# RWKV inputs: mixtures in the order of their use, r as plain fp32 products, three raw and three split weight buffers, finished chunks turned first

## Chip, cores and metric

The kernel runs on one core of a Trainium2 chip. The metric is the device time of one execution in microseconds (us), from the first to the last instruction with what lies around them; a kernel's figure is the median of its timed runs. TensorE has two clock levels, 1.2 and 2.4 GHz; the profile gives the granted clock of a stretch as a share of 2.4 GHz (1.00 or 0.50, and values between where a stretch holds both).

## The reference

Two blocks of two layers work on a sequence of 256 tokens by 1024 features, in float32. The first block (convolution mixer, cross attention, dense and mixture-of-experts feed-forward) and the first layer of the second block (attention, feed-forward) are untouched by the change. The change lies in the second layer of the second block, an RWKV-7 mixer that runs over the sequence in both directions:

```python
def rwkv7_mixer(h, ...):
    dx_p = jnp.pad(h, ((0, 0), (1, 0), (0, 0)))[:, :-1] - h
    dx_n = jnp.pad(h, ((0, 0), (0, 1), (0, 0)))[:, 1:] - h
    def mix(c):
        return h + dx_p * mu_prev[c] + dx_n * mu_next[c]
    xw, xa, xg = mix(1), mix(4), mix(5)
    r = mix(0) @ w_r
    k = mix(2) @ w_k
    v = mix(3) @ w_v
    kk = heads(k * k_k); kk = kk / norm(kk)
    for d in range(2):
        w_log = -softplus(-(w0[d] + tanh(xw @ w1[d]) @ w2[d])) - 0.5
        a = sigmoid(a0[d] + (xa @ a1[d]) @ a2[d])
        g = sigmoid(xg @ g1[d]) @ g2[d]
        ...   # scan over the tokens, group norm, bonus, times g
    y = dir_out[0] + dir_out[1]
    return y @ w_o
```

So six mixtures of the normalised input with its two neighbours feed six projections: k (mixture 2), the three low-rank ones w, a, g (mixtures 1, 4, 5), r (mixture 0) and v (mixture 3).

## The kernel before, in words

Features lie on the partitions, 8 tiles of 128 (`KD` = 8), and the 256 tokens in the free dimension. Weights stream from memory in raw chunks of 1024 KB into the pool `wst`.

There are two kinds of projections. A *split* one (`proj_T`, `proj`) cuts each operand in two fp32r parts, high and low, and makes three products for each (line 381); for that, ScalarE writes `wh` (line 344) and VectorE `wl` (line 345) from the raw chunk `wst`, which is free again then. A *plain* one (`plain_T`, line 514) multiplies the fp32 values in one go, with the raw chunk itself as operand, so that the chunk is free when TensorE has read it. The profile records a plain fp32 product of 128x256 as two matmul instructions.

In `rwkv_inputs` the normalised, transposed input is `hT`. A mixture for a plain projection is made by `whole`: for each of the 8 tiles one scaled copy on ScalarE (line 1431) and two multiply-adds on VectorE (line 1433) into `mx`. A mixture for a split projection is made by `mixed`: the same into `mixt` (lines 1444, 1446; four buffers of two tiles), then `mx_h` on ScalarE (line 1448) and `mx_l` on GpSimd (line 1449). The projections come in this order: k (plain), low-rank w (plain), r (split), group norms of k, low-rank a (plain), v (split), low-rank g (plain). After each pair of output tiles of k, ScalarE squares them (`ksq`, line 1461), TensorE sums the squares by group (line 1463), and VectorE and ScalarE write `z0` and `z1`. The order in which each engine issues its instructions comes from a planner that works on a simulated timeline; `high_priority` moves a block ahead in it, and `issue_after(ins)` queues the instructions of a block that run on the engine of `ins` behind `ins` in that engine's order (it adds no wait). `behind` does that for the instructions in the list `turned_all`, which `raw_T` sets.

The pool set `dense("c", 2, 4, "right", 3)` gives this stage two raw buffers `wst`, four each of `wh` and `wl`, and three of the mixture tiles.

After the inputs come the block stage (`rwkv_blocks`: VectorE and GpSimd products, lines 1572 to 1600), the inverses, and four steps of the scan. Step i handles chunk i of 64 tokens in one direction and chunk 3 - i in the other; `rwkv_norm` adds a chunk's normalised output to `y` (lines 1799 to 1801). So chunks 1 and 2 of `y` are complete after step 2, and chunks 0 and 3 after step 3. Then `y` is turned back to features on partitions by 128 small products with the identity (line 1394, `ps_tr`), split into `ry_h` and `ry_l` (lines 372, 373), and projected by `rk_o` (split, into `ps_acc`). The banks of PSUM are tagged: two `mm`, two `tr`, four `acc`; the scan's second direction uses `mm` and `tr`.

Of the kernel before, what the change touches and what calls it, by code (L numbers as in the profile page):

```python
# [15 lines left out]
OP = mybir.AluOpType  # L16
# [5 lines left out]
KD = 8  # L22
S = 256
# [191 lines left out]
class K:  # L215
# [1090 lines left out]
    def rwkv(self, h, hstack, hp):  # L1306
# [4 lines left out]
        nc, tc = self.nc, self.tc  # L1311
        with ExitStack() as ctx:
# [5 lines left out]
            with ExitStack() as left:  # L1318
                with ExitStack() as right:
                    rz = pool(right, "rwz", "right")  # L1320
                    rT, z0, z1 = (rz.tile([P, KD, S], F32, name=n) for n in ("rT", "z0", "z1"))
                    tT = rz.tile([65, 2, S], F32, name="tT")
                    aT = rz.tile([P, S], F32, name="aT")
                    nc.gpsimd.memset(tT[64:65], 1.0)
                    bq = pool(right, "rwq", "right")

                    def opened():
                        hstack.close()
                        lp = pool(ctx, "rwl", "left")
                        return lp, lp.tile([P, KD, 4, 64], F32, name="vx"), lp.tile([P, 2, S], F32, name="gT")  # L1330
                    with self.dense("c", 2, 4, "right", 3):
                        lp, vx, vm, gT = self.rwkv_inputs(h, rT, z0, z1, tT, aT, opened,
                                                      lambda lp: self.rwkv_low(bq, lp, 0, tT, aT))
                    cp = pool(left, "rwc", "left")
                    nt, pc, bon = ([cp.tile(sh, F32, name=f"{n}{d}") for d in range(2)] for n, sh in (
                        ("nt", [P, KD * 4, 64]), ("pc", [P, KD, 4]), ("bon", [P, KD, 4])))
                    xt = [cp.tile([P, KD * 4, 64], F32, name="xt0")]
                    ip = pool(left, "rwi", "left")
                    mp = pool(left, "rwm", "left", 2)
                    bp = pool(right, "rwb", "right")  # L1340
                    pads = [bp.tile([P, 4, 256], F32, name=f"pad{i}") for i in range(3)]
                    for t in pads:
                        nc.gpsimd.memset(t, 0.0)
                    for d in range(2):
                        sga = self.sga if d == 0 else self.rwkv_low(bq, lp, 1, tT, aT)
                        self.rwkv_blocks(bp, d, rT, z0, z1, pads, sga, nt[d], pc[d], bon[d], scr)
                    self.rwkv_inverse(ip, ip.tile([P, 3, 32, 32], F32, name="lanes", tag="lanes"), 0, nt[0], xt[0])
# [36 lines left out]
            with self.dense("d", side="right"):  # L1384
                yT = (self.xp.tile([P, KD, S], F32R, name="ry_h", tag="xT_h"),
                      self.xp.tile([P, KD, S], F32R, name="ry_l", tag="xT_l"))
                for f0 in range(0, KD, 2):
                    b = self.bank("tr")
                    for f in range(2):
                        for c in range(4):  # L1390
                            cs = slice(f * S + c * 64, f * S + c * 64 + 64)
                            for par in range(2):
                                src = slice(64 - 64 * par, 128 - 64 * par)
                                nc.tensor.matmul(b[64 * par:64 * par + 64, cs], y[src, f0 + f, c],  # L1394
                                                 self.ident[src, src], start=True, stop=True,
                                                 skip_group_check=True)
                    self.split(yT[0][:, f0:f0 + 2], yT[1][:, f0:f0 + 2], b.rearrange("p (f s) -> p f s", f=2))
                self.add_normed(self.wk, h, self.proj("rk_o", yT), self.norm2(1, 1))
        return h

    def rwkv_inputs(self, h, rT, z0, z1, tT, aT, opened, low):
# [3 lines left out]
        nc = self.nc  # L1405
        lo_, hi_ = slice(0, 64), slice(64, 128)
        with self.tc.tile_pool(name="rin", bufs=1, side="right", reuse_waits="tile") as mp:
# [20 lines left out]
            def whole(c):  # L1428
                x = self.xp.tile([P, KD, S], F32, name="mx", tag="xT_h")
                for q in range(KD):  # L1430
                    nc.scalar.activation(x[:, q], hT[:, q, 1:S + 1], AF.Copy, scale=mu0[:, c, q:q + 1])
                    for i, mu in ((0, mup), (2, mun)):
                        nc.vector.scalar_tensor_tensor(x[:, q], hT[:, q, i:i + S], mu[:, c, q:q + 1], x[:, q],
                                                       op0=OP.mult, op1=OP.add)
                return x

            def mixed(c):
# [18 lines left out]
            def ev_k(i, b):  # L1456
                nc.scalar.copy(z1[lo_, i:i + 2], b[lo_])
                nc.scalar.copy(z0[hi_, i:i + 2], b[hi_])
                for k in (i, i + 1):
# [4 lines left out]
                                         start=k + t == 0, stop=k == KD - 1, skip_group_check=True)  # L1464
                    for ps, z in ((lo_, z0), (hi_, z1)):
                        nc.vector.tensor_scalar(z[ps, k], b[ps, k - i], kg[ps, k:k + 1], None, op0=OP.mult)
            self.plain_T("rk_k", whole(2), 0, 8, ev_k)

            with self.tc.high_priority(400):
                r = self.rsqrt(pg[:, 0:32], 32, 1.0, 1e-30, op=OP.max)  # L1470
# [2 lines left out]
            def ev_w(i, b):  # L1473
                for d in range(2):
                    nc.scalar.activation(tT[0:64, d], b[64 * d:64 * d + 64, 0], AF.Tanh)
            self.plain_T("rk_l1", whole(1), 0, 1, ev_w)
            self.proj_T("rk_r", mixed(0), 0, 8, lambda i, b: nc.scalar.copy(rT[:, i:i + 2], b))
            for k0, pb in self.by_group(r):
                ks = slice(k0, k0 + 2)
                nc.vector.tensor_mul(z0[lo_, ks], z0[lo_, ks], pb[lo_])  # L1480
# [404 lines left out]
```

## Time and profile before

| | |
|---|---|
| median of 3 runs | 2659.81 us (2658.15 to 2661.5) |
| the profiled execution: its time | 2657.13 us |
| the profiled execution: span from first to last instruction | 2655.3 us |
| mean granted clock of TensorE | 0.949 |
| busy: TensorE, VectorE, ScalarE, GpSimd | 2451.8, 1994.8, 1548.3, 343.3 us |

All times of rows are microseconds from the span's start in that one execution. PE is TensorE (PEld its weight loads), DVE is VectorE, ACT is ScalarE, POOL is GpSimd, SPq the queue of SyncE that issues the transfers. A busy share over the whole span mixes stages with different limits, so stretches are read apart.

### The profile page before, as it was taken

The numbers are of one execution on the slowest core, as the hardware profiler recorded it, in microseconds if no ns is written. First come the engines' busy times: TensorE is split into PE (matmuls) and PEld (weight loads), VectorE is DVE, ScalarE is ACT, GpSimd is POOL, SyncE is SP. The second block draws the span as 40 slices with busy tenths as digits, with TensorE's granted clock in tenths as the row PEclk, the third lists the DMA queues.
The fourth block names the chain that finished last, engine by engine and source line by source line (L and its number), as shares of the span: only waits on it lengthen the run. The fifth ranks groups of instructions, "written<-read, shape, count | busy, mean of one in ns | idle before, by whom it ended". The sixth has DMA issues, their size and how long they took to land. (4 is left out here: it accounts for less than half of the span.)

```text
span 2655.3 us, 41131 instructions
## 1 busy us (share of the span) xinstructions
PE 2451.8 (92%) x15984; PEld 2102.2 (79%) x15984; DVE 1994.8 (75%) x2962; ACT 1548.3 (58%) x2168; POOL 343.3 (13%) x293
## 2 busy tenths in 40 slices
PE   8889999889999999999999999889899698687998
PEld 8778998778788888788888888677798576666897
DVE  8956556956689999888898989766655767867655
ACT  5445445335578777777777777645443446664443
POOL 3800110750000000000000000000011215500111
PEclk9989999899999999999999999989999799779999
DMA  6524454444489999999999999572453335735552
GB/s 243 169 103 148 163 190 164 139 148 175 135 316 368 348 362 353 353 347 358 350 359 345 353 362 362 185 258 80 140 186 104 129 121 126 189 126 203 175 188 98
DMA packets 229960, 598.83 MB, mean 226 GB/s; under 512 B 14779, under 2 KB 33915, under 8 KB 228477
## 3 DMA queue, kind: packets, MB, share of 16 engines
q1 hardware_dynamic: 229756, 596.12, 64.3%
q8 instruction: 127, 2.08, 0.3%
q14 instruction: 77, 0.62, 0.1%
HBM read 579.27 MB, written 16.81 MB: 224 GB/s over the span
## 5 line engine op out<-in xcount | busy, mean ns | idle before, releaser
L345 DVE TENSOR_TENSOR wl<-wst,wh 128x1024 fp32r<-128x1024 f32 (+2 forms) x1025 | 1227.9, 1227 | 347.8 <-ACT wh L344 339.8
L344 ACT ACTIVATE wh<-wst 128x1024 fp32r<-128x1024 f32 (+2 forms) x1025 | 1057.5, 1055 | 523.7 <-PE ps_mm L381 271.5
L381 PE MATMUL ps_mm<-xT_h,wh 128*128 128x256 f32 x1496 | 434.1, 290 | 28.4 <-DVE xT_l L460 15.4
L381 PE MATMUL ps_mm<-xT_h,wl 128*128 128x256 f32 x1496 | 431.2, 288 | 3.6 <-DVE wl L345 2.0
L381 PE MATMUL ps_mm<-xT_l,wh 128*128 128x256 f32 x1496 | 431.5, 288 | 0.2 <-DVE xT_l L460 0.2
L381 PE MATMUL ps_mm<-wh,gh 128*128 128x512 f32 x880 | 349.8, 398 | 0.0
L381 PE MATMUL ps_mm<-wl,gh 128*128 128x512 f32 x880 | 345.1, 392 | 0.0
L381 PE MATMUL ps_mm<-wh,gl 128*128 128x512 f32 x880 | 343.4, 390 | 0.0
L381 PEld LDWEIGHTS ps_mm<-xT_h,wh 128*128 128x128 f32 x1496 | 294.8, 197 | 35.6 <-DVE xT_l L460 16.3
L381 PEld LDWEIGHTS ps_mm<-xT_h,wl 128*128 128x128 f32 x1496 | 294.4, 197 | 7.1 <-DVE wl L345 4.3
L381 PEld LDWEIGHTS ps_mm<-xT_l,wh 128*128 128x128 f32 x1496 | 294.2, 197 | 1.1 <-DVE xT_l L460 0.4
L381 PEld LDWEIGHTS ps_mm<-wl,gh 128*128 128x128 f32 x880 | 165.3, 188 | 36.1
L381 PEld LDWEIGHTS ps_mm<-wh,gl 128*128 128x128 f32 x880 | 165.6, 188 | 32.9
L381 PEld LDWEIGHTS ps_mm<-wh,gh 128*128 128x128 f32 x880 | 165.5, 188 | 32.9
L381 PE MATMUL ps_acc<-wh,mal 128*128 128x512 f32 x448 | 179.0, 400 | 5.5 <-DVE mal L373 5.5
L381 PE MATMUL ps_acc<-wh,mah 128*128 128x512 f32 x448 | 177.7, 397 | 0.7 <-ACT mah L372 0.7
L381 PE MATMUL ps_acc<-wl,mah 128*128 128x512 f32 x448 | 177.6, 396 | 0.0
L1189 POOL MEMSET qz<- 64x2048 f32 x1 | 1.8, 1800 | 1156.3 <-DVEq L935 1156.3
L381 PE MATMUL ps_acc<-wh,al 128*128 128x512 f32 x344 | 134.8, 392 | 0.0
L381 PE MATMUL ps_acc<-wl,ah 128*128 128x512 f32 x344 | 134.5, 391 | 0.0
L1298 POOL TENSOR_TENSOR mq<-mr 128x512 f32<-128x512 f32 x32 | 55.2, 1729 | 582.0 <-DVE mr L1296 582.0
L381 PE MATMUL ps_acc<-wh,ah 128*128 128x512 f32 x344 | 115.9, 396 | 2.5 <-ACT ah L372 2.5
(484 smaller groups left out, 3846.2 us busy)
## 6 DMA issues: line engine op xcount, KB each, us to landing
wst<-in_moe_gate SPq DMA_DIRECT2D x112, 1024.0 KB, 7.0
wst<-in_moe_up SPq DMA_DIRECT2D x112, 1024.0 KB, 7.0
wst<-in_moe_down SPq DMA_DIRECT2D x112, 1024.0 KB, 6.5
wst<-in_mlp SPq DMA_DIRECT2D x64, 1024.0 KB, 4.8
wst<-in_mix_in SPq DMA_DIRECT2D x16, 1024.0 KB, 5.2
mc<-rwscr SPq DMA_DIRECT2D x8, 1792.0 KB, 7.2
wst<-in_ffn_gate SPq DMA_DIRECT2D x11, 1024.0 KB, 4.8
wst<-in_ffn_up SPq DMA_DIRECT2D x11, 1024.0 KB, 5.0
```

The lines of the kernel that those rows point to most:

```text
L344: nc.scalar.activation(wh[:, :n], src, AF.Copy)
L345: nc.vector.tensor_sub(wl[:, :n], src, wh[:, :n])
L381: self.nc.tensor.matmul(out, a, b, start=start and i == 0, stop=stop and i == n - 1, skip_group_check=True)
L1189: nc.gpsimd.memset(qz[64:128, :, 0], 0.0)
L1298: nc.gpsimd.tensor_mul(q, r, r)
```

## The change

Five things are changed. The mixture for k is made ahead under a raised priority, and the one for the low-rank w is traced before k's projection, in a block that queues its VectorE instructions behind the last VectorE step of k's mixture; r's mixture is queued in the same way behind that of w (`whole` now leaves its own last step in `turned_all`). r is a plain projection of a `whole` mixture in place of a split one. The pool set of the stage has three raw and three split buffers in place of two and four. The turn of `y` takes chunks 1 and 2 of all tiles first and chunks 0 and 3 after that, into four banks that are open at once, two tagged `tr` and two `mm`; the splits follow behind all turns in the text of the program. The mixtures of a, v and g are made as before.

```diff
-                    with self.dense("c", 2, 4, "right", 3):
+                    with self.dense("c", 3, 3, "right", 3):
...
-                for f0 in range(0, KD, 2):
-                    b = self.bank("tr")
-                    for f in range(2):
-                        for c in range(4):
-                            cs = slice(f * S + c * 64, f * S + c * 64 + 64)
+                bs = [self.bank(tag) for tag in ("tr", "tr", "mm", "mm")]
+                for cp in ((1, 2), (0, 3)):
+                    for f in range(KD):
+                        for c in cp:
+                            cs = slice(f % 2 * S + c * 64, f % 2 * S + c * 64 + 64)
                             for par in range(2):
                                 src = slice(64 - 64 * par, 128 - 64 * par)
-                                nc.tensor.matmul(b[64 * par:64 * par + 64, cs], y[src, f0 + f, c],
+                                nc.tensor.matmul(bs[f // 2][64 * par:64 * par + 64, cs], y[src, f, c],
                                                  self.ident[src, src], start=True, stop=True,
                                                  skip_group_check=True)
-                    self.split(yT[0][:, f0:f0 + 2], yT[1][:, f0:f0 + 2], b.rearrange("p (f s) -> p f s", f=2))
+                for f0 in range(0, KD, 2):
+                    self.split(yT[0][:, f0:f0 + 2], yT[1][:, f0:f0 + 2],
+                               bs[f0 // 2].rearrange("p (f s) -> p f s", f=2))
...
-                        nc.vector.scalar_tensor_tensor(x[:, q], hT[:, q, i:i + S], mu[:, c, q:q + 1], x[:, q],
-                                                       op0=OP.mult, op1=OP.add)
+                        last = nc.vector.scalar_tensor_tensor(x[:, q], hT[:, q, i:i + S], mu[:, c, q:q + 1], x[:, q],
+                                                              op0=OP.mult, op1=OP.add)
+                self.turned_all = [last]
                 return x
...
-            self.plain_T("rk_k", whole(2), 0, 8, ev_k)
+            with self.tc.high_priority(200):
+                first = whole(2)
+            with self.behind():
+                second = whole(1)
+            self.plain_T("rk_k", first, 0, 8, ev_k)
...
-            self.plain_T("rk_l1", whole(1), 0, 1, ev_w)
-            self.proj_T("rk_r", mixed(0), 0, 8, lambda i, b: nc.scalar.copy(rT[:, i:i + 2], b))
+            self.plain_T("rk_l1", second, 0, 1, ev_w)
+            with self.behind():
+                third = whole(0)
+            self.plain_T("rk_r", third, 0, 8, lambda i, b: nc.scalar.copy(rT[:, i:i + 2], b))
```

## Rows read from the trace of the kernel before

**Rows 1.** The head of the page and its first part: busy time and share.
```profile
span 2655.3 us, 41131 instructions
...
PE 2451.8 (92%) x15984; PEld 2102.2 (79%) x15984; DVE 1994.8 (75%) x2962; ACT 1548.3 (58%) x2168; POOL 343.3 (13%) x293
```

**Rows 2.** Busy time by engine in stretches of the inputs; then clock, DMA share, GB/s.
```profile
2072.00:2085.00 13.00, 5.21 (x13) 2.96 (x13) 13.00 (x34) 4.03 (x10) 8.73 (x1) 0.63 0.06 21
...
2125.00:2139.00 14.00, 8.44 (x42) 7.86 (x43) 11.73 (x23) 3.70 (x4) 4.68 (x4) 0.56 0.37 133
2139.00:2157.00 18.00, 18.00 (x153) 18.00 (x152) 7.24 (x6) 7.81 (x9) 0.00 (x0) 1.00 0.28 102
2157.00:2175.00 18.00, 18.00 (x86) 14.32 (x85) 15.74 (x30) 8.07 (x15) 1.89 (x2) 1.00 0.36 117
2175.00:2189.00 14.00, 14.00 (x56) 9.92 (x55) 4.63 (x8) 5.49 (x11) 0.00 (x0) 1.00 0.43 150
```

**Rows 3.** Timeline of TensorE: start, length, instructions [idle before, releaser].
```profile
2071.62 2.07 PE L514 MATMUL ps_mm<-mx,wst 128*128 128x256 f32 x4 [5.73 <-DVE mx L1433]
...
2076.37 1.13 PE L514 MATMUL ps_mm<-mx,wst 128*128 128x256 f32 x4 [0.31 <-DVE mx L1433]
2084.68 13.89 PE L514 MATMUL ps_mm<-mx,wst 128*128 128x256 f32 x52 [7.18 <-DVE mx L1433]
...
2107.57 7.15 PE L514 MATMUL ps_mm<-mx,wst 128*128 128x256 f32 x32
...
2122.23 0.62 PE L1463 MATMUL ps_tr<-cons,ksq 128*128 128x16 f32 x4 [1.51 <-ACT ksq L1461]
...
2131.72 0.58 PE L381 MATMUL ps_mm<-mx_h,wl 128*128 128x256 f32 x1 [3.33 <-DVE wl L345]
```

**Rows 4.** Waits of TensorE, 2065 to 2205: in total, times, longest.
```profile
PE ps_mm L514 <- DVE mx L1433: 13.5, 4, 7.2
PE ps_mm L381 <- ACT wh L344: 4.4, 2, 3.1
PE ps_mm L381 <- DVE wl L345: 3.3, 1, 3.3
PE ps_tr L1463 <- ACT ksq L1461: 2.6, 2, 1.5
```

**Rows 5.** Timeline of VectorE at the start of the inputs.
```profile
2068.32 0.87 DVE L1433 SCALAR_TENSOR_TENSOR mx<-hT,feats,mx 128x256 f32<-128x256 f32 x2
...
2077.03 3.64 DVE L1433 SCALAR_TENSOR_TENSOR mx<-hT,feats,mx 128x256 f32<-128x256 f32 x9
```

**Rows 6.** VectorE by line, 2065 to 2203: busy, mean ns, idle before.
```profile
L345 DVE TENSOR_TENSOR wl<-wst,wh 128x1024 fp32r<-128x1024 f32 x16 | 19.1, 1220 | 18.8 <-ACT wh L344 18.7
```

**Rows 7.** Transfers issued, 2040 to 2230: size, median us from issue to landing.
```profile
wst<-in_rk_v SPq DMA_DIRECT2D x4, 1024.0 KB, 4.9
```

**Rows 8.** The chain that ended last, 2420 to 2480: start, length, what.
```profile
2422.39 6.25 PE ps_tr L1394 x128
2428.64 22.00 PE ps_acc L381 x96
```

**Rows 9.** Timeline of SyncE's queue at the end of the scan.
```profile
2421.67 2.17 SPq L319 DMA_DIRECT2D wst<-in_rk_o  x4
```

**Rows 10.** Timeline of ScalarE behind the scan.
```profile
2426.63 2.01 ACT L344 ACTIVATE wh<-wst 128x1024 fp32r<-128x1024 f32 x2
```

**Rows 11.** The stretch ahead of the first `rk_o` product, columns as in the second group.
```profile
2426.00:2428.00 2.00, 2.00 (x51) 2.00 (x48) 0.97 (x2) 1.89 (x3) 0.00 (x0) 0.63 1.04 416
```

**Rows 12.** VectorE's products in the block stage, 2203 to 2310, by line and shape.
```profile
L1573 DVE TENSOR_TENSOR bk<-aw,zt 128x256 f32<-128x256 f32 x32 | 17.3, 569 | 0.2
...
L1575 DVE TENSOR_TENSOR pad<-z,e 64x256 f32<-64x256 f32 x16 | 12.8, 803 | 0.4
L1580 DVE TENSOR_TENSOR q<-bk,pad 64x256 f32<-64x256 f32 x16 | 11.1, 698 | 0.4
L1574 DVE TENSOR_TENSOR pad<-z,e 64x256 f32<-64x256 f32 x16 | 9.7, 604 | 5.9 <-issue 3.0 <-ACT e L1560 2.6
```

**Rows 13.** Timeline of GpSimd at the start of the inputs.
```profile
2076.27 11.07 POOL L1449 TENSOR_TENSOR mx_l<-mixt,mx_h 128x512 fp32r<-128x512 f32 x1 [30.09 <-ACT mx_h L1448]
```

## The prediction

> **What bounds the kernel now.** I first read the page: TensorE is busy 92% of a span of 2655.3 us [rows 1], but that is an average over stages. The change touches only the RWKV layer: the projections of `rwkv_inputs` and the turn of `y` ahead of `rk_o`. So I cut the first of these into stretches [rows 2]. From 2139 to 2189 TensorE is busy in every microsecond, at a granted clock of 1.00; it does r's products up to 2157, then group norms, v and small projections. Between 2072 and 2085 it works 5.21 of 13 us, between 2125 and 2139 8.44 of 14, at clocks of 0.63 and 0.56. These two holes are what the change can win; the 32 us after 2157 have none.
>
> The timeline of TensorE says what the holes are [rows 3]. Products of k start at 2071.62 and stop until 2084.68, waiting for VectorE's `mx`. Then they run densely; one chunk of 32 records takes 7.15 us, 0.223 us a record (two records make one fp32 product, here and in all that follows). The last small product after k and the first low-rank projection starts at 2122.23 and takes 0.62 us. Then r waits for split weights and gets going at 2131.72. The waits, summed, are 13.5 us for VectorE's `mx`, 4.4 for ScalarE's `wh` and 3.3 for VectorE's `wl` [rows 4]. The timeline of VectorE shows why the first wait exists [rows 5]: from 2068.32 on the steps of `mx` alternate with steps of `mixt`, and `mx` itself is two mixtures at once, so the one that k needs (16 steps) is spread over three mixtures' 48. One step takes 3.64/9 = 0.404 us when they stand back to back.
>
> **The change, part by part.** *The hold.* k's mixture is issued first, the mixture of the low-rank projection behind it on VectorE, r's behind that. 16 steps x 0.404 = 6.5 us from 2068.3: k's mixture is complete at 2074.8. TensorE can follow it, as it followed the scattered steps before. At 2074.8 all but the last 2 of the 16 records of the first output tile can be done, so 114 of k's 128 records are left. At 2084.68, before, 116 were left (three groups of 4 were done, two of them in [rows 3]). The old stretch from 2084.68 to 2122.85 takes 38.2 us: (116 + 16) x 0.223 = 29.4 us of products, and 8.8 us for the rise of the clock, group sums and waits for squares. I keep the 8.8: with 130 records the stretch takes 37.8 us and ends at 2112.6. Gain: 10.2 us. The hold binds only VectorE instructions; what is queued behind it there are the second and the third mixture, 32 steps or 12.9 us, wanted by TensorE only some 33 us later. v's mixture is not held; if it takes the place of r's old one, see the rivals.
>
> *r in plain products.* Removed: 192 products at 18.00/153 = 0.118 us each [rows 2], 22.6 us; the 8.8 us from 2122.85 to 2131.72, waits with two lone products within [rows 3, 4]; and what is left of the distance from 2122.85 to 2157, 2.7 us, for the dense products that still ran at half clock (0.56 in the mean between 2125 and 2139 [rows 2]). Together 34.1. Added: 64 products of 2 records, 128 x 0.223 = 28.5 us. So TensorE's own work grows by 5.9 us, and the stage still shrinks by 34.1 - 28.5 = 5.6. Eight conversions at 1.22 us on VectorE [rows 6], the eight on ScalarE and four subtractions on GpSimd go too; no later stage waited for them, so I count nothing. New end of r: 2112.6 + 28.5 = 2141.1, against 2157: **15.8 us** earlier.
>
> *Three raw and three split buffers.* A plain product holds its raw chunk until TensorE is done with it, where a split one gave it back after conversion. A fetch of one chunk takes 4.9 us to land [rows 7], and a chunk of r lasts 16 x 2 x 0.223 = 7.1 us. So even one chunk ahead is enough, and two are held. For v a chunk is 24 products of 512 columns, at 22.00/96 = 0.229 us [rows 8] 5.5 us; the fourth split buffer that goes would have been the tile after next, and a tile's conversion (1.22 us on VectorE) must fit in 2.75. Cost between 0 and 2 us (one fetch late by 4.9 minus the 3 us of small projections that can fill the place); I take 0, since in the old stretch, with two raw buffers, v ran without a hole.
>
> *The turn.* The 128 turns take 6.25 us behind the last step of `y` [rows 8]. Half of them now can precede it, 3.1 us. But the next step isn't free to follow: the fetch of `rk_o` is issued at 2421.67 [rows 9], and the first weights are converted at 2426.63, two in 2.01 us [rows 10], so `rk_o` can't begin before 2427.7, against 2428.64. Gain 0.9 at most. The price: the clock rose between 2426 and 2428 [rows 11], some 5 us after the turns began; with 2 us of idle TensorE ahead of `rk_o` it may rise up to 5 us later, half of which, 2.6 us, is lost. Net between -0.9 and +1.7; I take 0. The Trainium skill says the same in general ("TensorE: Matmul & The Clock Gate", Part 1): activity lifts the gate and idleness restores it. By that rule the sum would get the +1.7, by the old rise kept the -0.9.
>
> Sum: 15.8 us. What follows `rwkv_inputs` starts behind its last projection and moves as a whole. The profiled execution took 2657.13 us, of which 2655.3 are the span; it would take 2641. The median of the three runs stands 2.7 us above it, 2659.81, and my number is for a median: 2659.8 - 15.8 = 2644, less about 1 us for the waits for squares (2.6 us in all [rows 4], within the 8.8), which had mixtures in front of them: **2643**.
>
> **Rivals.** *The hold doesn't free VectorE.* v's mixture isn't held and shares the queue with k's. For it: that is how r's old one got in. Against it: k's is given priority, and its 16 steps depend on nothing that is late. Then k stays late, 10.2 us come back: 2653.
>
> *v starves.* v's raw chunks can be fetched only as r's give way. A chunk in series costs 4.9 us of fetch, 1.05 and 1.22 of conversion, 7.2 against 5.5 of products: 1.7 x 4 = 7 us lost, 2650. It turns into **slower** if these gaps also keep TensorE at half clock in v: its 96 products then take 22 us more, the loss is 29, and the time 2672. The point from which it decides is a loss of 15.8 + 5.3 = 21 us: the 7 and some two thirds of v at half clock. Against it: a chunk of r outlasts a fetch by 2 us, and the old v stage kept a clock of 1.00.
>
> *The block stage gives it back.* The order there is laid out anew by the planner. Its VectorE products of two SBUF tiles take 0.57 to 0.80 us in the mean depending on what GpSimd does beside them [rows 12]: 256 columns each, 50.9 us in all. If all took 0.803, 80 x 0.803 = 64.2: 13.3 us lost, 2656, no change. At `mx_l`, GpSimd took 11.07 us where it stood against VectorE's steps [rows 13]. For the gain on the other side there is as much room. The Trainium skill ("SBUF — State Buffer", Who interferes with whom) calls it an exclusive lock on a shared port pair, taken by whichever starts first. By that rule the order alone decides, and those rows agree; nothing in the diff changes this order directly.
>
> **How the numbers follow.** Something below 0.2%, 5.3 us, can't be told from no change here. The forecast has 0.68, with 2636 to 2648 as its own range (15.8 with up to 2 for v and 1.7 for the turn off, and up to 7 of the 8.8 us of clock and waits on top). The hold without effect 0.12, v starved at full clock 0.08 (2650), at half clock 0.05 (2672), the block stage 0.07 (2656). The range reaches from 2635 to 2654: it takes in the second and third. Faster: 0.68 + 0.08 + two thirds of 0.12, 0.84; same 0.10 (the block stage and the rest of the second); slower 0.06.
>
> **What would show it.** Right: k's products without a hole from about 2070 on, 130 records less than 40 us; r's first product within 1 us of the first low-rank projection, no `wh` of `rk_r`; r over some 16 us earlier than 2157; the first block product as much earlier; `rk_o` within 1 us of its old distance from the last `y` step. Wrong: `mixt` steps among k's `mx`; v with waits for `wst`; a granted clock under 1.00 between r and the blocks; VectorE's block products slower in the mean.

## The result, and the profile after

The changed kernel takes 2675.30 us (median of 4 runs, 2672.86 to 2677.74), the kernel before 2658.98 (4 runs): ratio 1.0056, 95% interval 1.0044 to 1.0069. It is **slower** by 0.56%; the forecast was faster, 2643 us, with 2636 to 2648 as its range. The profiled execution took 2672.86 us. The head of its page, beside [rows 1]:

```profile
span 2671.1 us, 40985 instructions
...
PE 2464.3 (92%) x15920; PEld 2112.2 (79%) x15920; DVE 1987.5 (74%) x2954; ACT 1537.5 (58%) x2156; POOL 328.5 (12%) x289
```

The stretches of the inputs, beside [rows 2], and TensorE's timeline, beside [rows 3]:

```profile
2072.00:2085.00 13.00, 7.62 (x18) 5.55 (x18) 13.00 (x34) 7.04 (x18) 0.00 (x0) 0.63 0.31 97
2125.00:2139.00 14.00, 14.00 (x67) 12.32 (x66) 4.17 (x15) 1.17 (x2) 1.46 (x2) 1.00 0.35 114
2139.00:2157.00 18.00, 18.00 (x86) 15.15 (x85) 8.52 (x18) 8.55 (x15) 0.00 (x0) 1.00 0.49 174
2157.00:2175.00 18.00, 18.00 (x79) 13.95 (x79) 13.41 (x17) 4.99 (x6) 1.90 (x2) 1.00 0.36 118
```

```profile
2070.49 5.70 PE L514 MATMUL ps_mm<-mx,wst 128*128 128x256 f32 x12 [4.15 <-DVE mx L1435]
2081.58 13.93 PE L514 MATMUL ps_mm<-mx,wst 128*128 128x256 f32 x52 [5.38 <-DVE mx L1435]
...
2119.01 0.62 PE L1466 MATMUL ps_tr<-cons,ksq 128*128 128x16 f32 x4 [1.50 <-ACT ksq L1464]
```

The second hole is closed: between 2125 and 2139 TensorE is busy throughout at a clock of 1.00. The first is not: the products of k still stop for 5.38 us. To see where time comes and goes, I measure from the first mixture step on VectorE (2068.32 before, 2068.77 after), in us. A place is where the instruction named starts, unless its end is named:

| up to | before | after | change |
|---|---|---|---|
| inputs' end (first write of the gate, `gT`) | 133.82 | 125.42 | -8.40 |
| first copy of the first inverse (`xt`) | 257.74 | 253.69 | -4.05 |
| its last copy ends | 271.38 | 274.13 | +2.75 |
| last copy of the second inverse ends | 301.46 | 299.22 | -2.24 |
| first new state of the scan (`sn`) | 306.05 | 308.15 | +2.10 |
| last sum of `y` | 352.64 | 364.98 | +12.34 |
| first product of `rk_o` | 360.25 | 371.98 | +11.73 |
| end of the span | 586.98 | 602.33 | +15.35 |

The inputs win 8.4 us, the inverses and the scan's first step give it all back and 2.1 more, the scan's other steps lose another 10.2, and what follows `rk_o`'s first product 3.6. With the 0.45 by which the first step itself is later, that is the 15.8 us between the two spans.

### The profile page after: what moved, and what is told of

The parts are those of the page before. It is cut to its first block, busy times and chain, and to the rows that moved or that the text cites. A ratio compares the mean times of both kernels' runs of the same rounds, so it can differ in the third digit from the quotient of the medians.

```text
span 2671.1 us, 40985 instructions
## 1 busy us (share of the span) xinstructions
PE 2464.3 (92%) x15920; PEld 2112.2 (79%) x15920; DVE 1987.5 (74%) x2954; ACT 1537.5 (58%) x2156; POOL 328.5 (12%) x289
## 5 line engine op out<-in xcount | busy, mean ns | idle before, releaser
L345 DVE TENSOR_TENSOR wl<-wst,wh 128x1024 fp32r<-128x1024 f32 x1017 | 1218.0, 1226 | 350.6 <-ACT wh L344 341.5
L344 ACT ACTIVATE wh<-wst 128x1024 fp32r<-128x1024 f32 x1017 | 1048.6, 1055 | 514.0 <-PE ps_mm L381 269.8
```

What stands on the lines that cost most here:

```text
L344: nc.scalar.activation(wh[:, :n], src, AF.Copy)
L345: nc.vector.tensor_sub(wl[:, :n], src, wh[:, :n])
```

## Experiments

The same distances are used below: *inputs* (their end), *first state*, *last y*, *rk_o*. Ratios are to the kernel before on the same chip.

| kernel | inputs | first state | last y | rk_o | ratio (95%) |
|---|---|---|---|---|---|
| before | 133.8 | 306.1 | 352.6 | 360.3 | 1 |
| after | 125.4 | 308.2 | 365.0 | 372.0 | 1.0056 (1.0044 to 1.0069) |
| e1_old_turn | 125.4 | 306.7 | 358.8 | 366.8 | 1.0026 (1.0016 to 1.0037) |
| e4_turn_behind | 125.4 | 308.7 | 362.1 | 368.7 | 1.0024 (1.0015 to 1.0033) |
| e2_turn_only | 133.9 | 306.7 | 353.0 | 359.8 | 1.0003 (0.9994 to 1.0012) |
| p_buf | 125.9 | 304.0 | 355.2 | 363.3 | 1.0004 (0.9995 to 1.0013) |
| p_rplain_buf | 125.6 | 303.6 | 353.6 | 361.2 | 1.0003 (0.9994 to 1.0012) |
| p_hold | 128.6 | 303.7 | 353.4 | 361.0 | 0.9990 (0.9981 to 0.9999) |
| e3_hold_all | 122.0 | 300.1 | 352.1 | 359.9 | 0.9994 (0.9985 to 1.0003) |
| e5_scan | 122.0 | 302.7 | 351.8 | 359.7 | 0.9986 (0.9977 to 0.9995) |
| e7_scan_sq | 121.8 | 304.8 | 354.9 | 362.2 | 0.9993 (0.9984 to 1.0002) |
| e8_hold_last3 | 125.3 | 304.4 | 351.8 | 359.8 | 0.9983 (0.9974 to 0.9992) |
| e9_step0_first | 122.1 | 295.3 | 347.1 | 354.7 | 0.9972 (0.9961 to 0.9984) |
| e10_best | 122.0 | 294.1 | 346.2 | 352.9 | 0.9976 (0.9967 to 0.9985) |

### The turn

**e1_old_turn**: the changed kernel with the old turn.

```diff
-bs = [self.bank(tag) for tag in ("tr", "tr", "mm", "mm")]
-for cp in ((1, 2), (0, 3)):
-    for f in range(KD):
-        for c in cp:
+for f0 in range(0, KD, 2):
+    b = self.bank("tr")
+    for f in range(2):
+        for c in range(4):
...
```

> The changed kernel with the old turn (f0 by f0, all four chunks, two tr banks); everything else of the change stays, and the order of the scan's other instructions is that of the changed kernel on every engine. Theory A (half of the turns stand in TensorE's queue inside the last scan step, wait there for the y of step 2, and hold up the step's products): the last y step comes 6.8 us behind the third again, as before, and not 12.8; 6 us come back, with up to 3 more in rk_o and its clock: 2666 to 2669. The first three y steps stay as late as in the changed kernel. Rival B (the turn's place costs nothing; the scan is late for its own new order): no change against the changed kernel, 2673 to 2677. Rival C (the turns are behind the whole of the scan's loss): 2661.

**e2_turn_only**: the kernel before with the new turn (the same diff the other way).

> The kernel before with the new turn alone. Here all turns stand behind the last scan product in TensorE's order, and the scan's order is that of before. Theory A (the place in the queue is the harm, not the new turn as such): 2659, within 2 us of before. Rival (the new turn is dear by itself, by four banks at once or by the splits behind all turns): 2665 or more.

**e4_turn_behind**: the changed kernel; every turn is put behind the scan's last TensorE product, in the order of issue alone.

```diff
+with self.tc.issue_after(scanned.ins):
     nc.tensor.matmul(bs[f // 2][64 * par:64 * par + 64, cs], y[src, f, c],
```

> The changed kernel, with its new turn queued behind the last product of the scan on TensorE. Theory A: as with the old turn, 2666 to 2669, within 2 us of it. Rival (four banks and late splits are the harm): 2673 or more, the old turn alone helps.

e1 took 2666.99 us, e4 2666.89, e2 2660.08 (before: 2660.52). Both ways of taking the turn out of the scan win back some 8 us, and the new turn alone costs nothing. TensorE's timeline of the changed kernel shows why, in the last step of the scan; then come VectorE's sums of `y` there, and the last two of the kernel before:

```profile
2422.35 0.34 PE L1394 MATMUL ps_tr<-ident,ry 64*64 64x64 f32 x1 [3.54 <-DVE ry L1810]
...
2422.52 1.49 PE L1768 MATMUL ps_mm<-rw,xt 64*64 64x64 f32 x24
...
2425.60 1.98 PE L1793 MATMUL ps_tr<-rs,mc 128*64 128x64 f32 x32
```

```profile
2390.24 1.28 DVE L1810 TENSOR_TENSOR ry<-ry,ro 128x512 f32<-128x512 f32 x2
2406.19 1.28 DVE L1810 TENSOR_TENSOR ry<-ry,ro 128x512 f32<-128x512 f32 x2
2420.92 1.28 DVE L1810 TENSOR_TENSOR ry<-ry,ro 128x512 f32<-128x512 f32 x2
2433.75 1.28 DVE L1810 TENSOR_TENSOR ry<-ry,ro 128x512 f32<-128x512 f32 x2
```

```profile
2414.12 1.28 DVE L1801 TENSOR_TENSOR ry<-ry,ro 128x512 f32<-128x512 f32 x2
2420.96 1.29 DVE L1801 TENSOR_TENSOR ry<-ry,ro 128x512 f32<-128x512 f32 x2
```

The first turn of chunks 1 and 2 (L1394) waits 3.54 us for the third sum of `y`, and in TensorE's one queue the last step's products (L1768) stand behind it. The last two sums are 12.8 us apart; before, they were 6.8 apart, in e1 and e4 8.1. The planner had put half of the turn into the step that it should have followed; in e2's order it did not, and the cost isn't there.

The stretches at the start of `rk_o`, each six microseconds ahead and four behind its first product, for before and then for e2 (columns as in [rows 2]):

```profile
2422.57:2428.57 6.00, 6.00 (x128) 5.93 (x128) 2.23 (x3) 3.06 (x5) 0.00 (x0) 0.59 0.95 354
2428.57:2432.57 4.00, 4.00 (x21) 3.31 (x19) 3.05 (x4) 2.58 (x5) 0.00 (x0) 1.00 1.04 417
```

```profile
2421.49:2427.49 6.00, 3.68 (x65) 3.50 (x65) 3.33 (x6) 3.47 (x6) 0.00 (x0) 0.50 0.82 299
2427.49:2431.49 4.00, 4.00 (x12) 3.20 (x13) 3.83 (x4) 2.92 (x4) 0.00 (x0) 0.64 1.04 417
```

With the new turn `rk_o` begins 0.9 us nearer to the last sum of `y` (6.8 us behind it for 7.6), but TensorE was busy only 3.68 us of the six ahead of it, and `rk_o` runs its first four at a mean clock of 0.64, where before they ran at 1.00: 12 products for 21. Both effects are those forecast. That their sum is no difference is partly luck: at the 0.229 us a product of [rows 8], nine products fewer are 2.1 us, more than the gain, and this loss is made up behind them, which the forecast did not count on. From `rk_o`'s first product to the end e2's profiled execution takes 226.5 us for 226.7. The changed kernel starts `rk_o` in the same way, at 0.60:

```profile
2440.75:2444.75 4.00, 4.00 (x11) 3.19 (x12) 3.85 (x4) 2.91 (x4) 0.00 (x0) 0.60 1.03 415
```

This agrees with the Trainium skill ("TensorE: Matmul & The Clock Gate", Part 1), by which activity lifts the gate and idleness restores it. The bound that the prediction set on the gain, the fetch of `rk_o`'s weights, held too: in the changed kernel's chain that ended last, `rk_o` waits for these weights, 5.11 us, not for the turn.

```profile
2434.46 5.11 DMA wst<-in_rk_o
...
2439.64 1.06 ACT wh L344
```

### The inputs, part by part

**p_buf**: the kernel before with three raw and three split buffers, nothing else.

```diff
-with self.dense("c", 2, 4, "right", 3):
+with self.dense("c", 3, 3, "right", 3):
```

> The kernel before with three raw and three split buffers and nothing else: the work of the inputs is that of before, but the order that the planner lays out for the inverse and the scan is another one (9 of the 16 first products of the first direction ahead of the second inverse, not 16; in the last scan step one product of the next step ahead of 16 that are ready). Theory B (the order is what costs): first mixture to last projection 134 us as before, but 64 to 68 us from the blocks' end to the first new state (before 60.5) and 49 to 52 us for the scan (46.6); the time is 5 to 12 us above before, 2666 to 2673. Rival (the buffers are free, and stages behind are late only where the inputs are early): within 2 us of before.

**p_rplain_buf**: the same with r in plain products.

```diff
-self.proj_T("rk_r", mixed(0), 0, 8, ...)
+self.plain_T("rk_r", whole(0), 0, 8, ...)
```

> The kernel before with r as plain fp32 products and three raw and three split buffers; mixtures and turn as before. My step for r: the inputs end 5.6 us earlier; if later stages shift as a whole, 2654 to 2655. Theory B (any shift of the inputs makes the planner lay out the inverse and the scan anew): in this kernel one product of the first direction's next step stands ahead of the second direction's 16 in the last step of the scan alone; 2 to 8 us of loss in inverse and scan, 2656 to 2662.

**p_hold**: the kernel before with the hold alone; r stays split.

```diff
+with self.tc.high_priority(200):
+    first = whole(2)
+with self.behind():
+    second = whole(1)
...
+with self.behind():
+    third = mixed(0)
```

> The kernel before with the hold alone, as the change has it: k's mixture first under priority, those of the low-rank w and of r queued behind it on VectorE; r stays split, buffers and turn stay as before. Theory A (the hold binds only the last traced VectorE step, and TensorE still waits for a late step of k's mixture): the inputs end 3 to 5 us earlier and not 10. Theory B (the planner then lays the inverse of the second direction and the scan out anew, which costs 5 to 10 us there): the time is 2659 to 2665, although the inputs are earlier. Rival (the hold works as I forecast, and later stages shift as a whole): 2650.

They took 2662.20, 2661.64 and 2658.72 us. The buffers alone shorten the inputs by 7.9 us, plain products then 0.3, the hold then 0.2; the hold alone 5.2. SyncE's queue shows what the third raw buffer does, first before, then p_buf:

```profile
2116.94 18.62 SPq L319 DMA_DIRECT2D wst<-in_rk_r  x4
```

```profile
2109.43 11.62 SPq L319 DMA_DIRECT2D wst<-in_rk_r  x4
```

r's fetches begin 7.5 us sooner, so its chunks are split before TensorE is free. (The expectation had put the inputs at 134 us, as before, and missed that.) Of the 7.7 us of waits for `wh` and `wl` [rows 4], p_buf's summed waits keep one of 1.2:

```profile
PE ps_mm L381 <- DVE wl L345: 1.2, 1, 1.2
```

In p_rplain_buf r is one dense run, nearly as long as forecast (27.89 us for 28.5):

```profile
2120.61 27.89 PE L514 MATMUL ps_mm<-mx,wst 128*128 128x256 f32 x128
```

So plain products have nothing left to win. The split's lone waits were a fetch begun too late, not a price of splitting.

Why does the hold add nothing on top? VectorE and ScalarE at the start of the changed kernel's inputs:

```profile
2068.77 0.48 DVE L1435 SCALAR_TENSOR_TENSOR mx<-hT,feats,mx 128x256 f32<-128x256 f32 x1
2069.17 0.48 DVE L1449 SCALAR_TENSOR_TENSOR mixt<-hT,feats,mixt 128x256 f32<-128x256 f32 x1
2069.56 0.87 DVE L1435 SCALAR_TENSOR_TENSOR mx<-hT,feats,mx 128x256 f32<-128x256 f32 x2
```

```profile
2067.36 0.49 ACT L1447 ACTIVATE mixt<-hT,mu 128x256 f32<-128x256 f32 x1
2067.76 1.29 ACT L1433 ACTIVATE mx<-hT,mu 128x256 f32<-128x256 f32 x3
```

`mixt` now belongs to v: `mixed(c)` takes its halves from four `mixt` buffers, r gave those up when it went to plain products, and v's mixture, which nothing holds, moves in at once. In p_hold, where r still uses them, VectorE's row is 32 steps of `mx` in one run, `mixt` comes behind it, and k's second stop is 1.46 us, not 5.38. One part of the change undoes another:

```profile
2068.32 13.11 DVE L1433 SCALAR_TENSOR_TENSOR mx<-hT,feats,mx 128x256 f32<-128x256 f32 x32
2081.34 6.42 DVE L1447 SCALAR_TENSOR_TENSOR mixt<-hT,feats,mixt 128x256 f32<-128x256 f32 x16
...
2077.13 11.49 PE L514 MATMUL ps_mm<-mx,wst 128*128 128x256 f32 x52 [1.46 <-DVE mx L1433]
```

But v is only half of it. By the profile, what ends k's second stop in the changed kernel is VectorE's 32nd mixture step. Of the 32, 8 are `mixt`, and as k's mixture has 16 steps, at least 8 more belong to w or r. In p_hold it is the 21st step, without any `mixt`, so at least 5 are not k's. The hold names one instruction, the last step of k's mixture in the text of the program. Read from these counts, the planner put that step ahead of another of k's, and steps of the next mixture between the two.

**e3_hold_all**: e1 with v's mixture held too, and all 24 steps of a mixture, ScalarE's among them, set as what the next one is queued behind.

```diff
-self.turned_all = [last]
+self.turned_all = steps
...
-acc = self.proj("rk_v", mixed(3))
+with self.behind():
+    fourth = mixed(3)
+acc = self.proj("rk_v", fourth)
```

> The changed kernel with the old turn and a hold that binds everything: the ScalarE copies of a mixture and all its VectorE steps are in the list that later mixtures wait behind, and v's mixture is held as well. Theory A (the hold failed since ScalarE's copies of four mixtures alternate and v's steps are not held): k's 16 steps are done by 2075 to 2076, its products run without the stop of 5.4 us, and the inputs end 5 to 8 us earlier than with the old turn alone; the time is 2659 to 2663 if the later stages only shift. Rival (k's mixture waits for something else, such as the transposed input): the stop stays, the time is that of the old turn alone. Rival (the planner lays the later stages out anew and eats it): inputs 5 to 8 us earlier and no change of the time.

2658.35 us. TensorE's and ScalarE's timelines:

```profile
2072.46 16.19 PE L514 MATMUL ps_mm<-mx,wst 128*128 128x256 f32 x64 [5.74 <-DVE mx L1434]
...
2114.67 1.04 PE L1465 MATMUL ps_tr<-cons,ksq 128*128 128x16 f32 x4 [4.30 <-ACT ksq L1463]
```

```profile
2108.18 3.29 ACT L1432 ACTIVATE mx<-hT,mu 128x256 f32<-128x256 f32 x8
2111.37 2.89 ACT L1446 ACTIVATE mixt<-hT,mu 128x256 f32<-128x256 f32 x7
2114.17 0.45 ACT L1463 ACTIVATE ksq<-ps_mm,feats 128x256 f32<-128x256 f32 x1
```

k's first 64 records now run without a hole. (In e8 below, with v held but only three of the 24 steps named, the stop is 2.52 us, and the 27th step ends it: so naming all steps counts beside holding v.) From the first mixture step to k's end it takes 40.9 us, for 52.1 before: 11.2 won, 10.2 forecast. But 15 copies of later mixtures (6.2 us) stand on ScalarE ahead of k's last squares, TensorE waits 4.30 for these, and the inputs end only 3.4 us sooner than in e1, where 5 to 8 were expected.

**e7_scan_sq**: e5 (below) with v's mixture also behind k's last square.

```diff
-with self.behind():
+with self.behind(), self.tc.issue_after(squared.ins):
```

> As the last one, and v's mixture is queued behind the last square of k on ScalarE as well. With the full hold alone, the last square waits behind 15 copies of other mixtures, and r starts 4.3 us late. Theory: the sums follow k at once, r starts 1 to 4 us earlier (its own copies move behind the squares as well). The order of the inverse that comes out has the gate products between the two inverses, as in the kernel before: if that order is what costs, inverse and gates take 56 to 57 us as before and not 61; then 2648 to 2652. If the loss there has another reason, 2653 to 2655.

2659.26 us, above both of the ranges expected; inputs 121.8 for 122.0. The wait of 4.30 us for the squares became one of 1.51, but behind it TensorE now waits 2.73 us for VectorE's `z`, and next to nothing was won.

### The order behind the inputs

Where the inputs end 8 to 12 us sooner, all or most of it is gone by `rk_o`, but for e9 and e10. One row of TensorE in e1 is typical of the scan:

```profile
2405.85 0.30 PE L1753 MATMUL ps_acc<-rs,mc 128*64 128x64 f32 x2 [3.01 <-issue]
2406.08 1.15 PE L1766 MATMUL ps_mm<-rw,xt 64*64 64x64 f32 x32
```

One direction's next-step products (L1753, which need VectorE's new state) stand ahead of the other direction's products with the inverse (L1766). The profile names no releaser here, but other rows do: VectorE begins to write the operand of L1753 at 2405.06, and that of L1766 was done by ScalarE at 2402.42. From the first state to the last sum of `y` the scan takes 46.6 us before, 52.1 in e1, 56.8 in the changed kernel.

**e5_scan**: e3; the first direction's next-step products are queued behind the second's products with the inverse.

```diff
+self.turned_all = [pul] if d == 1 else []
...
+with self.behind():
     last = nc.tensor.matmul(pw[own, f], mc[rows, f, 128 * par:128 * par + 64], ...)
...
```

> The changed kernel with the old turn, the full hold, and one more hold in the scan: the products of the first direction's next step are queued behind the second direction's products with the inverse on TensorE, as they stand in the kernel before. Theory B (one product of the next step, waiting for VectorE, stands in the queue ahead of 16 that are ready; TensorE idles 3 us there): 3 us less than without it, 2655 to 2656. Rival (VectorE's order, with the norm and the sum of the finished step ahead of the new state, sets the step): no change, 2658.

**e8_hold_last3**: e5 with the last three of a mixture's steps as the hold.

```diff
-self.turned_all = steps
+self.turned_all = [x for x in steps[-3:]]
```

> The changed kernel with the old turn and the hold in the scan, and later mixtures behind the last three instructions of the mixture ahead (its last ScalarE copy and both its last VectorE steps) in place of all 24. The order that the planner lays out in inverse, gates and scan is, by chance, nearly that of the kernel before (all 16 first products of the first direction, and its next step on ScalarE, ahead of the second inverse's end). Theory B: the inputs are as early as with the full hold, 10 to 12 us, inverse and gates take 60 to 62 us to the first new state, and most of the gain arrives: 2649 to 2653. Rival (the later stages are bound by something that doesn't move with the inputs, since five kernels with the inputs 5 to 12 us earlier all ended the scan at the same time from the first mixture): 2656 to 2660.

**e9_step0_first**: e5 with the scan's first step of the first direction raised, which needs the first inverse alone.

```diff
+if (i, d) == (0, 0):
+    ahead.enter_context(tc.high_priority(800))
 st[d], *o = self.rwkv_chunk(...)
```

> The kernel with the full hold, the old turn and the hold in the scan; the first direction's step 0 of the scan is raised in priority, so that its 16 products and the products with the first inverse stand ahead of the second inverse's tail, as in the kernel before. Theory B (that step 0 now waits for the whole second inverse costs 4 of the 9 us): the first new state comes 3 to 5 us earlier, 2652 to 2654. Rival (step 0 ahead delays the second inverse by as much): 2656 to 2658.

**e10_best**: e9 with the new turn, put behind the scan as in e4.

> The kernel with the full hold, the hold in the scan and the first step raised in priority (2653.1), with the new turn in place of the old one, queued behind the last product of the scan. The new turn so placed gained 1.3 us between the last sum of y and the first product of rk_o in the changed kernel, and 0.5 us in the kernel before: 2651.5 to 2653. Rival (no gain that arrives): 2653 to 2654.

e5 took 2656.87 us (before: 2661.24): the scan is 49.1 us long for e3's 52.0, but its first state comes 2.6 later. e8 took 2656.32, in the rival's range, with inputs 3.3 us longer than e5's: how early the inputs end hardly matters there. e9 took 2653.09 us, the best here: the first state comes 7.4 us sooner than in e5, and 4.7 of it arrive at the last sum of `y`, 5.0 at `rk_o`. (In the totals it is some 3.7, with intervals that overlap a little.) The rows are those of step 0's products with the first inverse, in e5 and then in e9:

```profile
2361.75 1.92 PE L1699 MATMUL ps_mm<-lxd,lz 32*32 32x32 f32 x64
...
2363.99 1.28 PE L1772 MATMUL ps_acc<-rw,xt 64*64 64x64 f32 x20
```

```profile
2338.24 1.97 PE L1775 MATMUL ps_acc<-rw,xt 64*64 64x64 f32 x32
```

Of these 16 products all stand behind the second inverse's last ones (L1699) in e5; in e9 all stand ahead, in the kernel before, e2 and e8 7, in the other kernels of the table but e10 none. e10 took 2654.47: `rk_o` begins 1.8 us sooner than in e9, but the new turn gains nothing that arrives there either.

### What the transfers do to the inverses

TensorE's timeline has idle time in the inverses that nothing in the profile releases ("issue"), after runs of 128 small products. In p_buf, with the stretch of one stall (columns as in [rows 2]; the last but one is the DMA share):

```profile
2316.02 1.05 PE L1669 MATMUL ps_mm<-lxd,lanes 32*32 32x16 f32 x64 [5.95 <-issue]
...
2350.08 1.90 PE L1669 MATMUL ps_mm<-lxd,lanes 32*32 32x16 f32 x128 [4.22 <-issue]
```

```profile
2310.10:2316.00 5.90, 0.00 (x0) 0.00 (x0) 4.10 (x13) 3.41 (x6) 2.38 (x4) 0.50 0.71 217
```

Before, these two stalls were 2.67 and 0.89 us. Four runs vary the transfers beside them.

**t1_buf_eighth**: p_buf with an eighth of the scan's matrices fetched; all heads then use the first head pair's matrices and inverse.

```diff
-nc.sync.dma_start(mc, scr[d, c])
+nc.sync.dma_start(mc[:, 0:1], scr[d, c, :, 0:1])
...
```

> The kernel before with three raw and three split buffers; each of the eight fetches of the scan's matrices brings an eighth (224 KB in place of 1792), and all heads use the matrices and the inverse of the first head pair, so the result is another one and only times are read. What is told apart: after the second inverse's first 122 products TensorE stands still for 3.8 to 4.9 us with no releaser in the five kernels where a fetch of these matrices was under way, and 0.4 to 1.6 us in six where it was not. Theory C (the stall is TensorE's own code, fetched in blocks of 16 KB beside the transfer): with an eighth of the bytes that stall falls to 0.4 to 2 us. Rival (the stall belongs to the place in the program, whatever moves beside it): 3.8 us or more remain. The order laid out for the scan differs in this kernel, so its whole time (2650 to 2662) decides nothing.

**t3_traffic**: the kernel before with four more copies of 1792 KB from DRAM to DRAM.

```diff
+for q in range(4):
+    nc.sync.dma_start(sink[q], scr[0, q])
```

> The kernel before with four extra copies in memory (each reads and writes 1792 KB there, nothing of it is used), issued behind the loads of the gates, so that transfers run through most of the inverses. In the kernel before TensorE's stalls without a releaser in the two inverses are 0.9 to 2.7 us each. Theory C (they are waits for its code, which comes beside the transfers): where the copies run, the stalls behind each block of 128 products grow to 4 to 6 us, and the inverses get 6 us longer or more. Rival (the stalls have nothing to do with transfers): 0.9 to 2.7 us each, as before. The order laid out behind the copies is another one, and the scan's own fetches wait behind them, so the whole time decides nothing; I expect it 10 to 40 us above before.

**t4_buf_late** and **e11_late**: p_buf and e9, with the fetches of the gate's weights (`g`, `gn`) held behind the first inverse's last sum, by small memsets into their tiles.

```diff
+with tc.issue_after(inverted.ins):
+    nc.vector.memset(g2[0:1, 0, 0:1], 0.0)
...
+            nc.vector.memset(t[64 * q:64 * q + 1, 0:1], 0.0)
```

> The kernel before with three raw and three split buffers, and the loads of the gates (1024 KB and four of 128 KB) held until the first inverse's last VectorE sum, by one small VectorE write into each of their tiles behind that sum. With the buffers alone TensorE stands still for 5.95 us without a releaser ahead of the last 64 products of the first inverse's third group, while these loads run; in the kernel before for 2.7. Theory C (a wait for its code, lengthened by the transfers beside it): the stall falls to 1.5 to 2.7 us, and the first inverse's copies come 3 to 4 us earlier. Rival (the place in the program makes the stall): 5 to 6 us remain. The gates get their data some 8 us later, so the end may not move: 2656 to 2662.

> The same hold of the gates' loads in the kernel with the full hold, the hold in the scan and the first step raised (2653.1). Theory C: its stall of 4.3 us in the first inverse falls below 2.7, the first inverse ends 2 us earlier. Whether that arrives depends on the order laid out behind it, in which step 0 stands less far ahead again (11 of 16 products ahead of the second inverse): 2650 to 2656. Rival: the stall stays, 2653 or more.

With the gate's fetches gone from beside it, the long stall of t4 is 1.57 us, at a DMA share of 0.02:

```profile
2312.88 1.05 PE L1675 MATMUL ps_mm<-lxd,lanes 32*32 32x16 f32 x64 [1.57 <-issue]
```

```profile
2311.30:2312.90 1.60, 0.03 (x6) 0.02 (x4) 1.60 (x1) 1.56 (x4) 1.55 (x3) 0.50 0.02 5
```

In e11 the same one falls from 4.32 to 2.12, in t1 the second from 4.22 to 1.02 (with another wait of 3.54 ahead of it there, so not a clean reading). The first inverse is copied out 1.4 us sooner in t4 (248.5 for 249.8) and 1.2 in e11 (245.3 for 246.5), of some 4 and 2 us that the stall lost; 3 to 4 and 2 were expected. The totals don't clearly follow: t4 2659.28 us, 0.9988 (0.9978 to 0.9998) for p_buf's 1.0004; e11 2660.17, 0.9995 (0.9984 to 1.0005), some 6 us worse than e9 and outside its range: the order changed again with the new writes (all of step 0's products with the inverse stand behind the second inverse, and its first state comes at 302.3, not 295.3). t1 took 2660.10, 0.9997 (0.9987 to 1.0006). t3 missed its dose: the planner issued the copies at 2251 us, ahead of the inverses, and a stall of 7.05 us stands where the DMA share is 0.63; it ran once, 2668.25 us beside 2658.34.

## Why the prediction was wrong

*The hold* (10.2 us): the failed step is "32 steps or 12.9 us, wanted by TensorE only some 33 us later", with k's 16 steps alone in front. k's mixture didn't get VectorE to itself: the step that TensorE waited for was the 32nd, not the 16th. This is the first rival, given 0.12. It named v's mixture, but not what let it in, the four `mixt` buffers that r's plain form had freed, and not the second way: a hold behind one step let steps of w or r in ahead of others of k's. The price was right: e3 wins 11.2 up to k's end.

*r in plain products* (5.6 us): 0.3 where the buffers are there. The 8.8 us that I took for a cost of the split was counted with the wrong part.

*Three raw and three split buffers* (0 us, down to a loss of 2): 7.9 us won by themselves. I asked what fewer split buffers might cost v and not what an earlier fetch gives r, though r's waits for `wh` were among my rows. v did run without a hole (TensorE busy 18.00 of the 18 us from 2157 on, at 1.00), so that rival fell; that its worst case, 2672, is close to the 2675.30 measured is chance.

In sum the inputs won 8.4 of 15.8 us. No run reached the 15.8: e3 won 11.8 with a wait of 4.30 in it, but e7, which shortened that wait, won 12.0.

*"What follows `rwkv_inputs` starts behind its last projection and moves as a whole"*: this is the step that cost most. From the inputs' end 10.5 us were lost up to the first state and 10.2 in the scan. The block stage's own rival fell as it was put: its VectorE products took 632, 769, 680 and 640 ns (before: [rows 12]), 52.7 us in all for 50.9, a loss of 1.8 and not of 13.3. The loss up to the first inverse is in the order and the stalls, by VectorE's transposition of its lanes, before and then after, and a row of TensorE after:

```profile
2285.06 2.06 DVE L1645 STREAM_TRANSPOSE lanes<-lanes 128x1024 f32<-128x1024 f32 x1
```

```profile
2290.89 2.04 DVE L1654 STREAM_TRANSPOSE lanes<-lanes 128x1024 f32<-128x1024 f32 x1
...
2307.00 0.30 PE L1664 MATMUL ps_mm<-lanes,nt 32*32 32x16 f32 x7 [3.19 <-issue]
```

It starts 5.8 us later, although the inputs end 8 us sooner, and the stall of 3.19 us stands at a DMA share of 0.97. From the inputs' end to the first state TensorE's waits for VectorE sum to 15.8 us before and 23.6 after, its stalls without a releaser to 12.3 and 15.0. No run tests that place by itself; it is read from rows. That the first step waits for the second inverse, and that the scan's order is worth microseconds, e9 and e5 show.

*The turn* (0 us): by its own terms right in the total, shown by e2 and e10, if partly by luck. The step left out was where its first half would stand in TensorE's queue: e1 and e4 both put that at 8 us. In the profiled executions of the changed kernel and e1, 4.7 of them are the scan's last step (12.8 for 8.1).

Still open: the 3.6 us that the changed kernel loses behind `rk_o`'s first product. The slow clock at its start isn't enough for them: e1, with the old turn, loses 2.0 there, and e2, with the new one, nothing. And since every edit lets the planner lay out the scan anew, the totals can't be split further.

## What to carry to other kernels

Where a planner orders instructions, an earlier start doesn't shift the rest: look at what stands ahead of what in the queue of the engine that sets the end, and raise the step whose inputs are ready first (e9, some 3.7 us on top of e5), or hold the one whose inputs are late (e4). A hold behind the last instruction in the program's text holds nothing that the planner puts ahead of the others: name them all (e3). Before pricing a part of a change, ask which buffers it frees and who takes them: the third raw buffer did r's work, and r's freed buffers undid the hold.

## What was not expected of the hardware

TensorE's stalls without a releaser depend on the transfers beside them. Over all 18 traces there are 129 such stalls of 0.85 us or more between 2284 and 2376 us. Each above 3.1 had transfers beside it, and with none (DMA share under 0.1) the longest was 2.71. Transfers alone don't make a stall long: at shares of 0.96 to 0.98 there are some of 1.50 to 1.77 (p_hold, t1, t3). From 2284 us to the last sum of `y` the stalls sum to 14.0 us before, to between 17.8 and 27.5 in the variants with earlier inputs, and to 11.7 in t4 (p_buf: 20.1).

The page's DMA part has a queue of instructions (this line is the changed kernel's), some 16 KB a packet:

```profile
q8 instruction: 127, 2.08, 0.3%
```

The times of its single packets are in the traces, and they fit a wait for code: 127 of the 129 stalls end 1.20 to 1.62 us after a packet of q8 has landed, but only 6 of the 61 waits of that length in the same stretches whose releaser the profile names. The two others are in e9 and e10, ahead of step 0's first products. p_buf's stall of 5.95 us ends 1.43 us behind a packet that began 5.15 us after the stall ahead of it; in t4, with the gate's fetches moved away, that packet began after 1.13 us, and the stall was 1.57. In e9 and e11 it is 3.76 and 1.67 us, with stalls of 4.32 and 2.12. By these rows TensorE waits there for what q8 brings, and the transfers beside it make that packet late, not long (p_buf's took 1.28 us, t4's 0.99). What in a transfer delays it, and how much of the loss behind the inputs these waits make, is not shown.
